# A hybrid decoder layer: normed rows and convolution channels turned from SBUF instead of through DRAM, and one tile's rows loaded into other buffers

## The chip, the core and the metric

The kernel runs on one core of a Trainium2 chip. The metric is the device time of one execution in microseconds (us); the time before is the median of three runs. The profile is one further execution of the same program, taken by the hardware profiler. Engines: PE is the matrix engine (TensorE), PEld its weight load, DVE the vector engine, ACT the scalar engine, POOL GpSimd; SP has no arithmetic here, it issues most of the DMAs. "SPq" and "ACTq" in the rows are DMA issues on the SP and ACT instruction streams. All data are 32-bit floats.

## The reference

One decoder layer on x with 2048 tokens and 1024 channels. What is computed, with the names of the stages that the kernel gives them:

```python
hn = rms_norm(x, mix_pre_g)                     # A
q, k, v, u = split(hn @ w_in)                   # A: 14 column blocks of 128
attn = sliding_window_attention(q, k, v, ...)   # B: window 128, 8 heads, sinks, bias
a, gate = split(u)                              # A
c = depthwise_conv31(a * sigmoid(gate))         # C, "taps": 31 taps, causal
c = silu(layer_norm(c, g, b))                   # C, "tail"
mixed = concat([attn, c @ w_conv_pw]) @ w_out   # W (w_conv_pw @ w_out is folded first, U)
h = x + rms_norm(mixed, mix_post_g)             # W, N
hn = rms_norm(h, ffn_pre_g)                     # N, then turned to channels-first, H
ff = (silu(hn @ w_gate) * (hn @ w_up)) @ w_down # F, then G
out = h + rms_norm(ff, ffn_post_g)              # G
```

layer_norm is over the 512 convolution channels of a token, rms_norm over the 1024 channels of a token.

## The kernel before, in words

**Tiles.** The 2048 tokens are four tiles t = 0 to 3 of 512. A weight or an activation is held as a pair (high part rounded to the fast matmul format, low part the rest), and each product is three matmuls (`three`, line 182; `product`, line 874). The feed-forward part is a seven-product scheme over pairs of tiles, first (0, 1), then (2, 3): names F0, G0, H0 in the code belong to the pair (0, 1), F2, G2, H2 to (2, 3).

**Order of the work.** The program writes its instructions from one main generator at a time (`run`, line 1345); each `yield c` of it lets the side generators in eight "lanes" (`Lane`, line 1267) advance by c times their rate, so that their instructions get their place among the main ones. The lanes that matter here: `lc` the taps T0 to T3 (with a priority that lies 100 places behind), `ld` the tails C0 and C1, `lw` the stages W0, then C2, W2, C3, W3, `lb` the attention B0 to B3, `lh` the turned operands H. The main line is A0, A1, A2, A3, then W1 with the first eight products of F0 inside it (`Q0`, line 1328), then F0, G0, F2, G2. `schedule_with_timeline_sim=True` (line 1493) then fixes the order of each engine's instructions at compile time; on the chip each engine runs its list in that order, and an instruction that waits holds all behind it on its engine. That holds for DMA issues on SP and ACT too.

**Buffers.** `BUFS` (line 53) gives each tag its number of SBUF buffers. Those that the change touches: `fc` 3 (512 values per partition; convolution values), `yt` 1, `chl` 5, `wx` 1, `mb` 2 (one holds the attention bias until B3 ends), `gb` 2, `fa` 4, `at` 2. In PSUM, `ct` is one bank, `tr` three, `mm` four. A new tile waits until the last reader of the buffer's former tile is done, a DMA from it included.

**Convolution.** `stage_taps` (line 554): for each of four channel blocks, 31 DVE instructions on one `fc` tile y, then SP stores y to DRAM (`y_scr`, line 565). `stage_tail` (line 568) loads each block back into an `fc` tile (line 577), turns it on PE to tokens-first in four 128x128 transposes into `ct` (line 549), and ACT copies it into the one `yt` tile (line 550). `conv_tail` (line 583) does the layer norm on `yt` in place (line 597), turns it back per channel block into `ct` (line 601), and makes two `fc` tiles from it: th = tanh (line 603) and v (line 605); DVE joins them (line 606), and SP stores v to `mixT` (line 607).

**Mixing products.** `stage_w(w)` (line 693) loads rows of `mixT` for tile w (`acts`, lines 699 to 711: group 0 is the attention half, the last group the convolution half), splits them into pairs on ACT (line 708) and DVE, and multiplies. For W1 both groups are loaded into `yt`, one 1 MB load each. Its products lie in `mm@W` (W0, W1) or `tr@W` (W2, W3).

**Norm and turn.** `norm_w` (line 747) makes h and the normed rows: xs, four `chl` tiles of 128 tokens x 1024 channels (line 781), which ACT stores to `hn_scr` (line 783). `stage_h_plain` (line 824) later loads a 512-token x 128-channel column block of them (`load_cols`, line 786, pieces of 512 bytes), turns it on PE into `ct` (line 810), scales it on ACT into a `gb` tile u (line 830), stores u to `hT` by a DMA issued on ACT (line 831), and splits u into a pair (lines 833 and 834), the operand `B11` (k = 0 to 3) or `B21` (k = 4 to 7) of the products. It runs for the even tile of each pair, 0 and 2. `stage_h_sums` (line 837) does the other operands: it loads u from `hT`, and the odd tile's blocks from `hn_scr` through `tr` banks.

Of the kernel before, what the change touches and what calls it, by code (L numbers as in the profile page):

```python
# [12 lines left out]
F32 = mybir.dt.float32  # L13
# [4 lines left out]
AF = mybir.ActivationFunctionType  # L18
ALU = mybir.AluOpType
# [6 lines left out]
P = 128  # L26
T = 512
NT = S // T
KC = D // P
# [8 lines left out]
def layer_kernel(ctx, tc, x, xT, cols, rows, sinks, relb, onehot, w_in, w_pw, w_out, w_gate, w_up, w_down, out):  # L38
    nc = tc.nc
# [15 lines left out]
    def t_(tag, shape, dt=F32):  # L55
        return sb.tile(list(shape), dt, tag=tag, name=nm(tag), bufs=BUFS[tag])
# [4 lines left out]
    def f2(tag, shape=(P, T)):  # L61
        return t_(tag, shape)
# [178 lines left out]
    glu_scr = dr.tile([4, P, S], F32, name="glu_scr")  # L241
    hn_scr = dr.tile([S, D], F32, name="hn_scr")
    y_scr = dr.tile([4, P, S], F32, name="y_scr")
    qs = {}
    started = set()

# [298 lines left out]
    def turner(yt, ycs):  # L545
# [5 lines left out]

        return turn

    def stage_taps(t):
        L = f"C{t}"
        for c in range(4):
            while f"g{t}{c}" not in started:
                yield None
            lab[0] = L
            g, y = conv_in(t, c)  # L560
            for j in range(1, TAPS):
                stt(y, g[:, j : j + T], dwh[:, c, j : j + 1], y, ALU.mult, ALU.add)
                yield 0.68
                lab[0] = L
            nc.sync.dma_start(y_scr[c, :, t * T : (t + 1) * T], y)
            yield 0.68

    def stage_tail(t):
        L = f"C{t}"
        lab[0] = L  # L570
        yt = t_("yt", (P, 4, 4 * P))
        ycs = []
        turn = turner(yt, ycs)
        for c in range(4):
            lab[0] = L
            y = f2("fc")
            nc.sync.dma_start(y, y_scr[c, :, t * T : (t + 1) * T])
            ycs.append(y)
            turn(c)
            yield 0.5  # L580
        yield from conv_tail(t, yt)

    def conv_tail(t, yt):
        L = f"C{t}"
        lab[0] = L
        mv = sm(8).rearrange("p (s a) -> p s a", a=2)
        for s in range(4):
            st = sm(6)
            nc.vector.bn_stats(st, yt[:, s])
            nc.vector.bn_aggr(mv[:, s], st)  # L590
        r = rsqrt(mv[:, :, 1], 4, 1.0)
        nmr = sm(4)
        stt(nmr, mv[:, :, 0], -1.0, r, ALU.mult, ALU.mult)
        yield YL if t < 2 else YL2
        lab[0] = L
        for s in range(4):
            act(yt[:, s], yt[:, s], AF.Identity, scale=r[:, s : s + 1], bias=nmr[:, s : s + 1])
        for c in range(4):
            b = ct()
            for s in range(4):  # L600
                nc.tensor.transpose(b[:, s * P : (s + 1) * P], yt[:, s, c * P : (c + 1) * P], ident)
            th = f2("fc")
            act(th, b, AF.Tanh, scale=lnh[:, c : c + 1], bias=lnh[:, 4 + c : 5 + c])
            v = f2("fc")
            act(v, b, AF.Identity, scale=lnh[:, c : c + 1], bias=lnh[:, 4 + c : 5 + c])
            stt(v, th, 1.0, v, ALU.add, ALU.mult)
            nc.sync.dma_start(mixT[4 + c, :, t * T : (t + 1) * T], v)
            yield YZ
            lab[0] = L

# [82 lines left out]
    def stage_w(w, atag, htags, rtags, bank_of, norm=None, ready=None):  # L693
        G = KC // len(htags)
        L = f"W{w}"
        lab[0] = L
        acc = [f4(atag) for _ in range(4)]

        def acts(gi):
            aa = []  # L700
            lab[0] = L
            n = 4 if rtags[gi] == "yt" else 2
            for c in range(G * gi, G * gi + G, n):
                ms = t_(rtags[gi], (P, n, T))
                nc.sync.dma_start(ms, mixT[c : c + n, :, w * T : (w + 1) * T].rearrange("c p t -> p c t"))
                for j in range(n):
                    a = hl(htags[gi])
                    act(a[:, 0], ms[:, j], AF.Copy)
                    vtt(a[:, 1], ms[:, j], a[:, 0].bitcast(F32), ALU.subtract)
                    aa.append([a])  # L710
            return aa

        def weights(gi, n):
            ws = []
            for c in range(G * gi, G * gi + G, 2):
                if c < 4:
                    ws += weight(w_out[c : c + 2, :, n * T : (n + 1) * T].rearrange("c p t -> p c t"), lo_out[n, c : c + 2], w > 0, on_pool=False)
                else:
                    for j in range(2):
                        ws.append(hl("w"))  # L720
                        nc.sync.dma_start(ws[-1].bitcast(F32), fold[n, c - 4 + j])
            return ws

        nxt = acts(0)
        yield W_LEAD
        for gi in range(KC // G):
            aa = nxt
            for n in range(2):
                lab[0] = L
                if n == 1 and gi + 1 < KC // G and not (ready and G * gi + G == 4):  # L730
                    nxt = acts(gi + 1)
                ws = weights(gi, n)
                yield from block_half(acc, list(zip(aa, ws)), n, gi == 0, L, bank_of)
            if ready and G * gi + G == 4:
                for i, c in enumerate(ready()):
                    if i == Q0 // 2:
                        ld.until("C1")
                        lab[0] = L
                        nxt = acts(gi + 1)
                    yield c  # L740
        tail = norm_w(w, acc)
        if norm:
            norm(tail)
        else:
            yield from tail

    def norm_w(w, acc):
        L = f"W{w}"
        lab[0] = L

        def whole(src):
            t = f4("chl")
            nc.sync.dma_start(t, src)
            return t

        gb = whole(rows[0].partition_broadcast(P))
        ssq = sm(4)
        for s in range(4):
            act(junk, acc[s], AF.Square, accum_out=ssq[:, s : s + 1])
            yield 0.75  # L760
            lab[0] = L
        r = rsqrt(ssq, 4, D, w < 3)
        xs = [whole(x[w * T + s * P : w * T + (s + 1) * P]) for s in range(4)]
        ssq2 = sm(4)
        yield 3
        for s in range(4):
            lab[0] = L
            stt(acc[s], acc[s], r[:, s : s + 1], gb, ALU.mult, ALU.mult)
            yield 1.25
            lab[0] = L  # L770
            vtt(acc[s], xs[s], acc[s], ALU.add)
            r0 = w * T + s * P
            nc.sync.dma_start(h_scr[r0 : r0 + P], acc[s])
            act(junk, acc[s], AF.Square, accum_out=ssq2[:, s : s + 1])
            yield 1.25
        lab[0] = L
        r2 = rsqrt(ssq2, 4, D, w < 3)
        yield 3
        for s in range(4):
            lab[0] = L  # L780
            act(xs[s], acc[s], AF.Copy, scale=r2[:, s : s + 1])
            r0 = w * T + s * P
            nc.scalar.dma_start(hn_scr[r0 : r0 + P], xs[s])
            yield 1.25

    def load_cols(w, k, tag):
        t = f2(tag, (P, 4, P))
# [18 lines left out]
    def turned(w, k, bank_of, tag):  # L806
        c = load_cols(w, k, tag)
        b = bank_of()
        for s in range(4):
            nc.tensor.transpose(b[:, s * P : (s + 1) * P], c[:, s], ident)  # L810
        return b
# [12 lines left out]
    def stage_h_plain(ws, ops, n, off):  # L824
        L = f"H{ws[0]}"
        for k in range(4):
            lab[0] = L
            b = turned(ws[0], k + off, ct, COLTAG[ws[0]][k] if ws[0] else "fa")
            u = f2("gb")
            act(u, b, AF.Copy, scale=g_ffn[:, k + off : k + off + 1])  # L830
            nc.scalar.dma_start(hT[ws[0] // 2][k + off], u)
            o = op_tile(ws, ops, n, k, {})
            act(o[:, 0], u, AF.Copy)
            lo(u, o, False)
            yield 2.0
# [509 lines left out]
    def run(gen):  # L1345
        for c in gen:
            clk[0] += c
            for lane in lanes:
                lane.pump(c)
# [52 lines left out]
            hn_a[t + 1] += split_x(t + 1, xa[t + 1][0], xa[t + 1][2], range(4, KC))  # L1402
    lw.until("W0")
    mids = [dr.tile([7, NF // 2, P, T], F32, name=f"mids{i}") for i in range(2)]
    hT = [dr.tile([KC, P, T], F32, name=f"hT{i}") for i in range(2)]
    td = dr.tile([4, NF // 2, P, T], F32, name="td")
    keeps = [dr.tile([PRES[2 * i], P, T], F32, name=f"keeps{i}") for i in range(2)]
    ws, ops = (0, 1), {}
    for n, off in (("B11", 0), ("B21", 4)):
        lh.add(n + ".0", stage_h_plain(ws, ops, n, off))  # L1410
    run(stage_w(1, "mid", ["hl", "chl"], ["yt", "yt"], mm, norm=lambda g: lh.add("N1", g), ready=lambda: stage_pre(ws, ops, mids[0], keeps[0], 0, Q0)))
    lc.hold = lambda: "S0" not in lh.done
    lh.until("B21.0")
    lh.add("S0", stage_h_sums(ws, ops), lambda: f"P0.{PRE_S0}" in started and "B3" in lb.done)
# [83 lines left out]
```

## Time and profile before

| | us |
|---|---|
| median of 3 runs | 1991.65 |
| lowest, highest run | 1988.4, 1992.08 |
| the profiled execution's own time | 1988.67 |
| its span, first to last instruction | 1986.6 |
| PE busy | 1930.2 (97%) |
| DVE busy | 1460.2 (73%) |
| ACT busy | 955.2 (48%) |
| DMA, moved in all | 454.56 MB, mean 229 GB/s |
| mean granted TensorE clock | 0.992 |

How to read it: a matmul of 512 columns is listed with some 390 ns, but successive ones overlap, so the number of matmuls that start in a window says more than their busy time: in an undisturbed 10 us about 46 start. "Idle" of PE is time in which none is in flight. The granted clock in a window is 1.00 when the throttle passes everything. In a row of the time line stand the start, the length, the engine, the line, the operation, out<-in, the count, and in brackets the idle time of the engine just before with what ended it. In a row of waits stand the total, the number and the longest wait. In a row of DMA issues stand the count, the size of one and the median time from issue to landing. A row of windows has the stretch, its length, then for each engine the busy time with the number of instructions, then the granted clock, the DMA engines' busy share and GB/s.

### The profile page before, as it was taken

To read this page: it belongs to the slowest core of one execution; us is meant where nothing else is said; L and a number is where in the kernel's file an instruction comes from. 1 tells how busy PE (TensorE), PEld (TensorE's weight loads), DVE (VectorE), ACT (ScalarE), POOL (GpSimd) and SP (SyncE) were. 2 spreads that over 40 slices of the span, in tenths; PEclk is the share of its full clock that TensorE was granted. 3 is DMA by queue.
4 is the path that set the end of the run, shared out by engine and by line. 5 is a ranking of instruction groups with operands and counts; after the bars stand their busy time and mean duration, and the time that the engine had idled before them with its cause. 6 is when DMAs were issued, how large, how long until landed. Compare 5 with 4: busy or idle time off the path is not lost.

```text
span 1986.6 us, 26669 instructions
## 1 busy us (share of the span) xinstructions
PE 1930.2 (97%) x8730; PEld 1542.3 (78%) x8730; DVE 1460.2 (73%) x2578; ACT 955.2 (48%) x1878; POOL 336.4 (17%) x415
## 2 busy tenths in 40 slices
PE   8999999998999999899999999989999999999997
PEld 6777767776777778778888778768888888888886
DVE  5999969986875898888658975766666665455557
ACT  5455454436737633334355466556634433345443
POOL 4011111003121200000000110144423332311003
PEclk9999999999999999999999999989999999999999
DMA  8797757669659867885477788797844542466664
GB/s 312 253 316 234 228 176 242 213 198 306 203 191 353 290 216 237 285 267 181 154 236 251 266 302 282 270 315 244 289 149 165 170 164 81 143 232 194 210 196 144
DMA packets 229403, 454.56 MB, mean 229 GB/s; under 512 B 22632, under 2 KB 48400, under 8 KB 229264
## 3 DMA queue, kind: packets, MB, share of 16 engines
q1 hardware_dynamic: 211024, 426.64, 64.5%
q10 hardware_dynamic: 18240, 26.22, 3.6%
q8 instruction: 69, 1.13, 0.2%
q14 instruction: 70, 0.57, 0.1%
HBM read 331.65 MB, written 121.12 MB: 228 GB/s over the span
## 4 chain that ended last, share of the span: by engine, by line
PE 43%; DMA 10%; DVE 9%; issue 3%; POOL 2%; ACT 2%; SPq 1%; DVEq 0%; ACTq 0%; POOLq 0%
PE mm@F L85 29%; PE mm@G L85 12%; DVE fc@C L94 2%; PE tr@W L85 2%; DMA gb@F<-keeps 1%; DVE hl@G L94 1%; DMA mids<-fa@F 1%; DMA fa@G<-mids 1%; DMA td<-fc@G 1%; DVE w@F L94 1%; DMA fc@G<-w_down 1%; DMA wx@G<-w_down 1%; DVE fa@F L94 1%; DVE chl@F L94 1%; DMA mixT<-fc@C 1%
## 5 line engine op out<-in xcount | busy, mean ns | idle before, releaser
L94 DVE SCALAR_TENSOR_TENSOR fc@C<-glu@C,colt,fc@C 128x512 f32<-128x512 f32 x480 | 356.5, 760 | 2.9
L85 PE MATMUL mm@F<-hl@H,w@F 128*128 128x512 f32 x1056 | 253.0, 390 | 3.3 <-ACT mm@F L919 2.0
L85 PE MATMUL mm@G<-hl@G,hl@G 128*128 128x512 f32 x924 | 232.6, 397 | 11.2 <-ACT hl@G L792 7.7
L85 PEld LDWEIGHTS mm@F<-hl@H,w@F 128*128 128x128 f32 x1056 | 197.5, 188 | 46.3 <-ACT mm@F L919 3.7
L85 PEld LDWEIGHTS mm@G<-hl@G,hl@G 128*128 128x128 f32 x924 | 173.0, 190 | 51.7 <-ACT hl@G L792 9.0
L85 PE MATMUL mm@A<-hl@A,w@A 128*128 128x512 f32 x840 | 206.5, 395 | 4.2 <-ACT w@A L127 1.9
L792 ACT ACTIVATE w@F<-chl@F 128x512 fp32r<-128x512 f32 x220 | 135.4, 625 | 142.1 <-PE mm@F L85 131.5
L85 PE MATMUL mm@G<-w@G,hl@G 128*128 128x512 f32 x876 | 199.4, 389 | 0.0
L85 PEld LDWEIGHTS mm@G<-w@G,hl@G 128*128 128x128 f32 x876 | 164.4, 188 | 34.1
L85 PEld LDWEIGHTS mm@A<-hl@A,w@A 128*128 128x128 f32 x840 | 155.4, 188 | 42.2 <-ACT w@A L127 2.6
L94 DVE TENSOR_TENSOR w@F<-chl@F,w@F 128x512 fp32r<-128x512 f32 x198 | 144.8, 735 | 35.9 <-ACT w@F L792 35.3
L85 PE MATMUL mm@F<-ql@H,w@F 128*128 128x512 f32 x528 | 128.4, 391 | 9.2 <-ACT mm@F L1026 5.0
L85 PE MATMUL mm@F<-mid@H,w@F 128*128 128x512 f32 x528 | 131.7, 396 | 0.0
L85 PE MATMUL mm@F<-p@H,w@F 128*128 128x512 f32 x528 | 129.4, 390 | 0.0
L85 PE MATMUL mm@F<-x@H,w@F 128*128 128x512 f32 x528 | 125.7, 391 | 0.0
L85 PEld LDWEIGHTS mm@F<-ql@H,w@F 128*128 128x128 f32 x528 | 98.8, 188 | 31.6 <-ACT mm@F L1026 6.4
L494 POOL TENSOR_SCALAR_AFFINE_SELECT p@B<-p@B 128x512 f32<-128x512 f32 x62 | 57.6, 938 | 374.0 <-ACT p@B L492 372.7
L85 PEld LDWEIGHTS mm@F<-mid@H,w@F 128*128 128x128 f32 x528 | 100.0, 190 | 21.9 <-ACT fa@F L1047 0.5
L85 PEld LDWEIGHTS mm@F<-p@H,w@F 128*128 128x128 f32 x528 | 99.5, 188 | 21.0 <-ACT at@F L1040 0.2
L85 PEld LDWEIGHTS mm@F<-x@H,w@F 128*128 128x128 f32 x528 | 98.6, 188 | 21.5 <-issue 0.8
L127 ACT ACTIVATE w@A<-raw@A 128x512 fp32r<-128x512 f32 x110 | 67.4, 625 | 93.5 <-PE mm@A L85 54.8
L94 DVE TENSOR_TENSOR w@G<-raw@G,w@G 128x512 fp32r<-128x512 f32 x73 | 51.5, 705 | 68.1 <-ACT w@G L792 66.8
(302 smaller groups left out, 3300.6 us busy)
## 6 DMA issues: line engine op xcount, KB each, us to landing
mids<-fa@F SPq DMA_DIRECT2D x154, 256.0 KB, 2.8
raw@A<-w_in SPq DMA_DIRECT2D x55, 512.0 KB, 4.7
w@A<-lo_in SPq DMA_DIRECT2D x84, 256.0 KB, 3.6
fc@G<-mids SPq DMA_DIRECT2D x77, 256.0 KB, 3.5
fa@G<-mids SPq DMA_DIRECT2D x75, 256.0 KB, 4.6
gb@F<-keeps SPq DMA_DIRECT2D x72, 256.0 KB, 3.9
w@W<-fold SPq DMA_DIRECT2D x32, 512.0 KB, 5.1
chl@F<-w_gate SPq DMA_DIRECT2D x22, 512.0 KB, 4.1
```

The costliest lines, as they stand in the source:

```text
L85: r = nc.tensor.matmul(*args, **kw)
L94: r = op(*args, **kw)
L127: act(w[:, 0], raw, AF.Copy)
L494: nc.gpsimd.affine_select(out=pg[:, kb].rearrange("p (i q) -> p i q", q=P), in_=pg[:, 1].rearrange("p (i q) -> p i q", q=P), compare_op=AL ...
L792: act(w[:, 0], x, AF.Copy)
```

## The change

Four things are altered.

1. **Convolution channels, tiles 0 and 1.** `stage_taps` no longer stores y to DRAM: as soon as a channel block's taps are done, it turns y into the `yt` tile (taken at the tile's first block, `turns[t]`), in the `lc` lane. `stage_tail(0)` and `(1)` then start with the layer norm. Tiles 2 and 3 still go through `y_scr`.
2. **The tail's values.** In `conv_tail`, for all tiles, v is written into the slice of `yt` that it came from, not into an `fc` tile; the store to `mixT` reads from there, four pieces of 512 bytes per partition.
3. **Normed rows, tiles 0 and 2.** They are no longer stored to `hn_scr` and loaded back in columns. For tile 0 `stage_h_plain` turns them straight from the `chl` tiles, by the new `turn_row`, and `lh.until("B21.0")` in W1 sees to it that this is placed before W1's second group takes `chl` tiles. For tile 2 `norm_w` itself turns all eight blocks and stores them to `hT`, with 2.0 of lane time each, and `stage_h_plain` loads u from `hT`.
4. **Tile 1's rows.** W1's first group goes into a `wx` and an `mb` tile, 512 KB each; the second stays in `yt`.

```diff
--- before.py
+++ after.py
@@ -241,6 +241,7 @@
     glu_scr = dr.tile([4, P, S], F32, name="glu_scr")
     hn_scr = dr.tile([S, D], F32, name="hn_scr")
     y_scr = dr.tile([4, P, S], F32, name="y_scr")
+    hT = [dr.tile([KC, P, T], F32, name=f"hT{i}") for i in range(2)]
     qs = {}
     started = set()
 
@@ -551,6 +552,8 @@
 
         return turn
 
+    turns = {}
+
     def stage_taps(t):
         L = f"C{t}"
         for c in range(4):
@@ -562,12 +565,20 @@
                 stt(y, g[:, j : j + T], dwh[:, c, j : j + 1], y, ALU.mult, ALU.add)
                 yield 0.68
                 lab[0] = L
-            nc.sync.dma_start(y_scr[c, :, t * T : (t + 1) * T], y)
+            if t < 2:
+                if c == 0:
+                    turns[t] = t_("yt", (P, 4, 4 * P))
+                turner(turns[t], {c: y})(c)
+            else:
+                nc.sync.dma_start(y_scr[c, :, t * T : (t + 1) * T], y)
             yield 0.68
 
     def stage_tail(t):
         L = f"C{t}"
         lab[0] = L
+        if t < 2:
+            yield from conv_tail(t, turns[t])
+            return
         yt = t_("yt", (P, 4, 4 * P))
         ycs = []
         turn = turner(yt, ycs)
@@ -601,10 +612,11 @@
                 nc.tensor.transpose(b[:, s * P : (s + 1) * P], yt[:, s, c * P : (c + 1) * P], ident)
             th = f2("fc")
             act(th, b, AF.Tanh, scale=lnh[:, c : c + 1], bias=lnh[:, 4 + c : 5 + c])
-            v = f2("fc")
-            act(v, b, AF.Identity, scale=lnh[:, c : c + 1], bias=lnh[:, 4 + c : 5 + c])
-            stt(v, th, 1.0, v, ALU.add, ALU.mult)
-            nc.sync.dma_start(mixT[4 + c, :, t * T : (t + 1) * T], v)
+            v = yt[:, :, c * P : (c + 1) * P]
+            four = lambda a: a.rearrange("p (s c) -> p s c", c=P)
+            act(v, four(b), AF.Identity, scale=lnh[:, c : c + 1], bias=lnh[:, 4 + c : 5 + c])
+            stt(v, four(th), 1.0, v, ALU.add, ALU.mult)
+            nc.sync.dma_start(four(mixT[4 + c, :, t * T : (t + 1) * T]), v)
             yield YZ
             lab[0] = L
 
@@ -701,7 +713,7 @@
             lab[0] = L
             n = 4 if rtags[gi] == "yt" else 2
             for c in range(G * gi, G * gi + G, n):
-                ms = t_(rtags[gi], (P, n, T))
+                ms = t_(rtags[gi][c // 2 % 2] if isinstance(rtags[gi], tuple) else rtags[gi], (P, n, T))
                 nc.sync.dma_start(ms, mixT[c : c + n, :, w * T : (w + 1) * T].rearrange("c p t -> p c t"))
                 for j in range(n):
                     a = hl(htags[gi])
@@ -735,6 +747,7 @@
                 for i, c in enumerate(ready()):
                     if i == Q0 // 2:
                         ld.until("C1")
+                        lh.until("B21.0")
                         lab[0] = L
                         nxt = acts(gi + 1)
                     yield c
@@ -779,9 +792,28 @@
         for s in range(4):
             lab[0] = L
             act(xs[s], acc[s], AF.Copy, scale=r2[:, s : s + 1])
-            r0 = w * T + s * P
-            nc.scalar.dma_start(hn_scr[r0 : r0 + P], xs[s])
+            if w % 2:
+                r0 = w * T + s * P
+                nc.scalar.dma_start(hn_scr[r0 : r0 + P], xs[s])
             yield 1.25
+        if w == 0:
+            normed.extend(xs)
+        if w == 2:
+            for k in range(KC):
+                turn_row(w, xs, k)
+                yield 2.0
+
+    normed = []
+
+    def turn_row(w, xs, k):
+        lab[0] = f"H{w}"
+        b = ct()
+        for s in range(4):
+            nc.tensor.transpose(b[:, s * P : (s + 1) * P], xs[s][:, k * P : (k + 1) * P], ident)
+        u = f2("gb")
+        act(u, b, AF.Copy, scale=g_ffn[:, k : k + 1])
+        nc.scalar.dma_start(hT[w // 2][k], u)
+        return u
 
     def load_cols(w, k, tag):
         t = f2(tag, (P, 4, P))
@@ -825,10 +857,12 @@
         L = f"H{ws[0]}"
         for k in range(4):
             lab[0] = L
-            b = turned(ws[0], k + off, ct, COLTAG[ws[0]][k] if ws[0] else "fa")
-            u = f2("gb")
-            act(u, b, AF.Copy, scale=g_ffn[:, k + off : k + off + 1])
-            nc.scalar.dma_start(hT[ws[0] // 2][k + off], u)
+            if ws[0]:
+                u = f2(COLTAG[ws[0]][k])
+                nc.sync.dma_start(u, hT[ws[0] // 2][k + off])
+            else:
+                u = turn_row(0, normed, k + off)
+                lab[0] = L
             o = op_tile(ws, ops, n, k, {})
             act(o[:, 0], u, AF.Copy)
             lo(u, o, False)
@@ -1402,13 +1436,12 @@
             hn_a[t + 1] += split_x(t + 1, xa[t + 1][0], xa[t + 1][2], range(4, KC))
     lw.until("W0")
     mids = [dr.tile([7, NF // 2, P, T], F32, name=f"mids{i}") for i in range(2)]
-    hT = [dr.tile([KC, P, T], F32, name=f"hT{i}") for i in range(2)]
     td = dr.tile([4, NF // 2, P, T], F32, name="td")
     keeps = [dr.tile([PRES[2 * i], P, T], F32, name=f"keeps{i}") for i in range(2)]
     ws, ops = (0, 1), {}
     for n, off in (("B11", 0), ("B21", 4)):
         lh.add(n + ".0", stage_h_plain(ws, ops, n, off))
-    run(stage_w(1, "mid", ["hl", "chl"], ["yt", "yt"], mm, norm=lambda g: lh.add("N1", g), ready=lambda: stage_pre(ws, ops, mids[0], keeps[0], 0, Q0)))
+    run(stage_w(1, "mid", ["hl", "chl"], [("wx", "mb"), "yt"], mm, norm=lambda g: lh.add("N1", g), ready=lambda: stage_pre(ws, ops, mids[0], keeps[0], 0, Q0)))
     lc.hold = lambda: "S0" not in lh.done
     lh.until("B21.0")
     lh.add("S0", stage_h_sums(ws, ops), lambda: f"P0.{PRE_S0}" in started and "B3" in lb.done)
```

## The prediction

> **What bounds the kernel now.** I read the page first, for the bound and the chain of work that ended last.
>
> ```profile
> span 1986.6 us, 26669 instructions
> PE 1930.2 (97%) x8730; PEld 1542.3 (78%) x8730; DVE 1460.2 (73%) x2578; ACT 955.2 (48%) x1878; POOL 336.4 (17%) x415
> ...
> PEclk9999999999999999999999999989999999999999
> ...
> PE 43%; DMA 10%; DVE 9%; issue 3%; POOL 2%; ACT 2%; SPq 1%; DVEq 0%; ACTq 0%; POOLq 0%
> ```
>
> The matrix engine is the bound: it sits idle for only 1986.6 - 1930.2 = 56.4 us. The change leaves every matmul and every transpose in place, so it can win only from these 56 us and from stretches in which PE's clock was cut. I therefore looked, by windows of 10 us, for where PE loses.
>
> ```profile
> 480.00:490.00 10.00, 5.87 (x37) 4.62 (x35) 6.27 (x11) 4.53 (x8) 0.00 (x0) 0.90 1.04 398
> 490.00:500.00 10.00, 8.55 (x39) 7.13 (x40) 9.96 (x33) 2.99 (x9) 0.00 (x0) 0.76 0.82 247
> ...
> 810.00:820.00 10.00, 5.97 (x20) 4.46 (x19) 8.14 (x15) 2.67 (x5) 0.00 (x0) 0.83 0.91 328
> 870.00:880.00 10.00, 6.21 (x22) 4.76 (x21) 9.65 (x17) 1.67 (x3) 0.00 (x0) 0.85 0.78 255
> 1310.00:1320.00 10.00, 3.50 (x13) 2.56 (x12) 4.05 (x7) 4.62 (x12) 4.60 (x8) 0.70 1.08 368
> 1320.00:1330.00 10.00, 10.00 (x42) 8.07 (x42) 9.20 (x16) 5.65 (x12) 9.50 (x16) 0.79 0.62 193
> 1350.00:1360.00 10.00, 10.00 (x46) 8.28 (x45) 9.79 (x19) 4.62 (x10) 4.96 (x5) 1.00 0.62 194
> ```
>
> The last row is the undisturbed rate. Two holes lie where the change works: 480 to 500 (A3 gives way to W1) and 1310 to 1330 (tile 2's turned operands). The pair at 810 and 870 lies in F0, which the change doesn't touch. In each of the four the clock falls below 1.00, so a hole costs more than its idle time. The first costs (10 - 5.87) + (10 - 8.55) = 5.6 us idle, and by clock 0.10 x 5.87 + 0.24 x 8.55 = 2.6 us: **8.2 us**. The second costs 6.5 us idle and 0.30 x 3.50 + 0.21 x 10 = 3.2 us: **9.7 us**.
>
> The Trainium skill (TensorE: Matmul & The Clock Gate, the HAM clock gate) says that after an idle window of about 3.4 us the clock halves until about 3.4 us of work have passed; that would be about 1.7 us a hole as an estimate. By it the sum below would gain some 2 us less. The clock rows here give 2.6 and 3.2.
>
> The time line tells what ended the first hole:
>
> ```profile
> 480.55 0.37 SPq L705 DMA_DIRECT2D yt@W<-mixT  x1
> 483.66 0.55 DVE L94 TENSOR_SCALAR fc@C<-glu@C,colt 128x512 f32<-128x512 f32 x1 [7.43 <-DMA mixT<-fc@C]
> 484.78 1.08 PE L85 MATMUL tr@B<-kz,ql@A 64*128 64x256 f32 x13
> 490.69 2.19 ACT L708 ACTIVATE hl@W<-yt@W 128x512 fp32r<-128x512 f32 x4 [4.69 <-DMA yt@W<-mixT]
> 491.45 1.65 PE L85 MATMUL tr@B<-kz,ql@A 64*128 64x256 f32 x12 [5.59 <-DVE sm@B L454]
> 493.03 7.45 PE L85 MATMUL mm@W<-w@W,hl@W 128*128 128x512 f32 x28
> ```
>
> PE ends the projections and a part of B3's scores at 485.86 and then stands before the next scores, which wait for DVE. DVE is late because a tap's first instruction stood 7.43 us before a free `fc` tile: the tail C1 had all three, and one was still being stored to `mixT`. W1 would not have filled the hole either: its rows go into `yt`, which C1 held, so the load was issued at 480.55 and ACT split it at 490.69. Both causes are buffer waits, and DMA is full (1.04).
>
> The second hole:
>
> ```profile
> 1304.05 1.44 SPq L1133 DMA_DIRECT2D mb@G<-w_down  x2
> 1305.54 0.47 SPq L1129 DMA_DIRECT2D fa@G<-mids  x1
> 1306.06 0.45 SPq L1102 DMA_DIRECT2D chl@G<-h_scr  x1
> 1306.99 4.83 PE L85 MATMUL mm@G<-hl@G,hl@G 128*128 128x512 f32 x20
> 1308.79 0.67 ACT L830 ACTIVATE gb@H<-ct@H,colt 128x512 f32<-128x512 f32 x1
> 1315.01 0.33 ACTq L831 DMA_DIRECT2D hT<-gb@H  x1
> 1315.38 0.63 ACT L1094 ACTIVATE junk<-p@G 128x512 bf16<-128x512 f32 x1 [5.92 <-DMA chl@G<-h_scr]
> 1318.33 8.49 PE L85 MATMUL mm@G<-hl@G,hl@G 128*128 128x512 f32 x24 [6.50 <-ACT hl@G L792]
> ```
>
> ACT ends u at 1309.46, then its store to `hT` isn't issued until 1315.01, held by the `chl@G` load of 1306.06. Behind that store in ACT's order stand the splits `hl@G` that PE waits for.
>
> **The change part by part.** The DMAs, from the issues with size and landing time, and the rows for the moved steps:
>
> ```profile
> hn_scr<-chl@W ACTq DMA_DIRECT2D x16, 512.0 KB, 6.7
> y_scr<-fc@C SPq DMA_DIRECT2D x16, 256.0 KB, 3.3
> fc@C<-y_scr SPq DMA_DIRECT2D x16, 256.0 KB, 4.8
> mixT<-fc@C SPq DMA_DIRECT2D x16, 256.0 KB, 5.2
> hT<-gb@H ACTq DMA_DIRECT2D x16, 256.0 KB, 4.4
> fa@H<-hn_scr SPq DMA_DIRECT2D x8, 256.0 KB, 6.0
> ```
> ```profile
> PE ct@C L549 <- DMA fc@C<-y_scr: 1.4, 2, 1.0
> ```
> ```profile
> SPq L565 <- DVE fc@C L94: 25.7, 12, 4.5
> ```
> ```profile
> L491 PE MATMUL tr@B<-ident,p@B 128*128 128x128 f32 x128 | 20.3, 278 | 0.0
> ...
> L810 PE MATMUL ct@H<-ident,fa@H 128*128 128x128 f32 x32 | 5.3, 279 | 0.0
> ```
> ```profile
> 284.06 0.61 DVE L94 TENSOR_SCALAR fc@C<-glu@C,colt 128x512 f32<-128x512 f32 x1 [5.69 <-DMA mixT<-fc@C]
> ```
> ```profile
> L810 PE MATMUL ct@H<-ident,fa@H x32: 270/272/329, 500.7 to 545.3; 128*128 128x128 f32 x32
> L830 ACT ACTIVATE gb@H<-ct@H,colt x16: 668/684/692, 503.4 to 1308.8; 128x512 f32<-128x512 f32 x16
> ```
> ```profile
> L85 PE MATMUL mm@W<-w@W,chl@W x96: 387/389/496, 560.2 to 587.2; 128*128 128x512 f32 x96
> ```
>
> *Traffic.* Gone are 8 stores of 512 KB to `hn_scr`, 16 column loads, 8 stores and 8 loads of `y_scr` at 256 KB; new are 8 loads from `hT`. That is 4 + 4 + 2 + 2 - 2 = 10 MB of 454.56. At the mean of 229 GB/s it is some 45 us of transfer, but PE is the bound, so I count it at nothing by itself; it thins the queues at just the two holes, where DMA reads 1.04 and 1.08. PE's 64 + 64 transposes and ACT's copies stay, only moved.
>
> *W1's rows and the tail's values (first hole).* `wx` is W0's and long done with; `mb`'s second buffer is free too. Their loads need not wait for C1, so I expect them to land well before 485, and W1's products to stand ready when A3 ends. With v in `yt`, C1 needs one `fc` tile per block rather than two, so the tap takes its tile without the 7.43 us, and the scores come in time. ACT's 2.19 us of splits move ahead into a fuller stretch. Bounds: nothing (something else holds W1) and 8.2 us; I take 7.2, leaving 1 us for a late weight: the cover, both causes lifted at once, is good. The same removal lifts 5.69 us of DVE wait at 284; PE wasn't waiting there, so that counts at nothing, but it gives DVE room.
>
> *Tile 2's rows (second hole).* In the stretch 1300 to 1316 no store of u is left on ACT, so the 5.92 us stand goes. Next late are the loads themselves: `fa@G`, issued at 1305.54, with DMA full. If it takes the 9 us that the load of 1306.06 took, PE starts near 1316 and wins 2.4 us; if it lands in time, the whole 9.7 us go. Between these I take 6. In return `norm_w(2)` gets eight blocks at once near 1175: each has an ACT copy of 0.68 and a DMA issue of 0.33, 8 us of ACT, through the single `ct` bank, and the splits `hl@G` stand behind them. Such turns cost PE no idle so far (0.0 over 32). Bounds 0 and 8 x 0.68 = 5.4; I take 1. The lane time of 16 doesn't move C3: by the code's own costs C2, W2 and the turns end at (26 + 45.6 + 24 + 16) / 1.25 = 89, and T3's taps let C3 start at 124 x 0.68 / 0.9 + 10 = 104.
>
> *Tile 0's rows.* The turn needs no DMA, so B11 and B21 (500.7 to 545.3 now) come earlier. The added order holds W1's second group until `chl` is free; it is used only at 560, so 15 us remain even at the old times: nothing.
>
> *Turns inside the taps.* Eight times PE now waits for DVE itself instead of a load. The two old waits, 1.4 us, go. Behind a waiting transpose stand the projections, so a late tap stops PE. What speaks to its price: PE's transposes of what DVE just made in B cost 0.0 idle over 128; SP, placed at the same taps' ends, waited 25.7 / 12 = 2.1 us each. Bounds 0 and 8 x 4.5 = 36 us. I take 3 us, near the B row, which is PE's own. A second wait, for which the stores of C0 are the row:
>
> ```profile
> L607 SPq DMA_DIRECT2D mixT<-fc@C x4: 319/320/384, 268.8 to 292.4; - x4
> ```
>
> T1's first block finds `yt` with C0 until the last of these has landed, 292.4 + 5.2. An ACT copy placed before that stops the weight splits behind it, and by them PE; the order of the lists should put it later, so I count it within the 3.
>
> *Sum:* -7.2 - 6 - 1.4 + 1 + 3 = -10.6 us against the profiled execution's own 1988.67 (span 1986.6 and 2 us around it): 1978. The median of the runs is 3 us above that execution and the runs spread over 3.7; I add 2: **1980 us**.
>
> **The rivals.**
> *The second hole stays.* ACT's stand only moves: DMA at 1.08 keeps the loads late, or the eight stores near 1175 meet the same kind of hold. For it: the transfers of h, `mids` and `w_down` remain. Then 6 us of gain go: 1986.
> *It doesn't do what it says at W1.* The order of the lists is fixed at compile time; if W1's loads stand behind other SP issues, or B3's scores still wait for DVE, the hole keeps its size, and the second too: -1.4 + 4 on 1988.67, with 2 us as above: about 1993. Against it: two causes would have to return.
> *Slower: PE stands before the taps.* One mechanism, at the eight turns of T0 and T1, in A1 to A3, where DVE runs full. At SP's mean of 2.1 us it costs 17, at its longest 36; it decides from (7.2 + 6 + 1.4 - 1) / 8 = 1.7 us a turn. At 3.3 us it is 26: 1988.67 - 13.6 + 26 + 2 = 2003. For it: SP's waits. Against it: SP is mostly idle and waits wherever it stands; PE has a backlog.
>
> **How the numbers follow.** Forecast 0.45, the second hole stays 0.17 (both faster by over 0.2%, about 4 us, which is what a measurement of this kernel can tell from no change), nothing happens at W1 0.13 (same), slower 0.25. So faster 0.62, same 0.13, slower 0.25. The range: both holes gone whole and the turns for nothing give 1988.67 - 17.9 - 1.4 + 2 = 1971, less the runs' spread of 3.7 is 1967; up to 2002, which takes in the middle cases and the lower half of the slow one. The forecast's own range is 1967 to 1985.
>
> **What would show it.** First hole: no PE idle above 2 us and a clock of 1.00 between A3's end and W1; rows of `wx@W` and `mb@W` landing before. No `fc@C` tap waiting for `mixT`. Second: no `hT` store on ACT near 1300, idle under 3 us. Turns: PE's `ct@C` transposes at the taps with less than 1 us of idle each. The forecast is wrong if PE waits for `fc@C` on DVE add up to over 13 us, if a new hole of over 3.8 us opens near 1175, or if F0's holes at 810 and 870 grow by shifted work.

## The result and the profile after

The changed kernel takes 1998.71 us (median of 11 runs, 1994.5 to 2004.8) against 1989.81 us (11 runs, 1986.41 to 1992.08): ratio 1.0051, 95% interval 1.0038 to 1.0063. It is **slower** by about 9 us, little but clear of the noise, where 10 us faster was forecast. The profiled execution took 1997.41 us.

The page of the changed kernel:

```profile
span 1995.4 us, 26645 instructions
...
PE 1933.4 (97%) x8730; PEld 1547.1 (78%) x8730; DVE 1465.0 (73%) x2578; ACT 952.6 (48%) x1878; POOL 327.0 (16%) x415
...
PE   8999999999998999999999999996999999999997
...
PEclk9999999999999999999999999998999999999999
...
DMA packets 224811, 444.06 MB, mean 223 GB/s; under 512 B 22137, under 2 KB 47905, under 8 KB 224673
```

The 10 MB are gone as reckoned, and PE's work is the same 8730 matmuls. But PE's row has a 6 in its 28th slice, where before no slice but the last is under 8. The windows of the changed kernel (stretch, length, busy time of PE, PEld, DVE, ACT and POOL with instructions, clock, DMA share, GB/s):

```profile
480.00:490.00 10.00, 10.00 (x60) 7.51 (x60) 4.19 (x18) 6.93 (x10) 0.00 (x0) 1.00 0.44 131
490.00:500.00 10.00, 10.00 (x54) 7.87 (x53) 9.93 (x26) 8.77 (x27) 0.00 (x0) 1.00 0.57 172
810.00:820.00 10.00, 10.00 (x46) 8.28 (x45) 9.39 (x16) 4.97 (x10) 0.00 (x0) 1.00 0.87 294
870.00:880.00 10.00, 10.00 (x44) 8.17 (x44) 8.99 (x16) 4.91 (x9) 0.00 (x0) 0.96 0.81 262
1310.00:1320.00 10.00, 10.00 (x46) 8.29 (x45) 9.69 (x17) 3.42 (x7) 0.00 (x0) 1.00 0.75 279
1320.00:1330.00 10.00, 10.00 (x46) 8.29 (x45) 8.11 (x14) 9.08 (x21) 5.68 (x5) 1.00 0.98 351
1350.00:1360.00 10.00, 5.60 (x22) 3.97 (x22) 6.42 (x17) 5.20 (x15) 5.32 (x12) 1.00 0.98 351
1360.00:1370.00 10.00, 8.48 (x30) 6.35 (x30) 9.91 (x16) 5.02 (x12) 6.94 (x8) 0.83 0.98 328
1370.00:1380.00 10.00, 5.70 (x22) 4.48 (x23) 5.04 (x17) 2.65 (x5) 0.00 (x0) 0.83 1.01 321
1380.00:1390.00 10.00, 5.26 (x17) 3.58 (x16) 5.83 (x8) 5.03 (x10) 2.24 (x2) 0.81 1.05 357
1390.00:1400.00 10.00, 7.42 (x24) 5.69 (x24) 4.54 (x4) 4.99 (x10) 5.93 (x5) 0.68 0.74 246
1400.00:1410.00 10.00, 6.13 (x28) 4.72 (x27) 7.74 (x9) 6.39 (x12) 4.68 (x3) 0.83 0.61 195
1410.00:1420.00 10.00, 10.00 (x40) 8.09 (x39) 8.07 (x9) 6.34 (x13) 7.74 (x7) 0.83 0.67 216
```

Both holes of the forecast, 480 to 500 and 1310 to 1330, are filled at full clock, and F0's two at 810 and 870 have no idle time either. A new one has opened at F2's start, from 1350 to 1420. A count in these rows takes in every matmul that has a part in the window, so two neighbouring windows share the one at their border. The rate at which matmuls start undisturbed is nearer 44 in 10 us than 46 (146 in 33.25 us in this kernel's time line from 1316.69 on). From 1350 to 1420, as one window, there are 176 matmuls where 7 x 44 = 308 would be; the 132 missing are 132 x 10 / 44 = **30 us**. Of these 21.4 us are idle time (70 less 48.59 busy). The busy time of each row times what its clock lacks to 1.00 adds up to 8.5 us, which is the rest. DMA's share is 0.98 to 1.05 up to 1390.

Why there? N3, the norm of tile 3, ends much later. These are the last stores of h, in the rows of the tile `h_scr` from 1000 to 1450, first of before:

```profile
L773 SPq DMA_DIRECT2D h_scr<-mid@W x8: 319/320/438, 1145.5 to 1284.0; - x8
L1102 SPq DMA_DIRECT2D chl@G<-h_scr x8: 319/326/479, 1277.4 to 1334.4; - x8
```

and then of the changed kernel:

```profile
L786 SPq DMA_DIRECT2D h_scr<-mid@W x8: 319/320/358, 1135.2 to 1322.3; - x8
L1136 SPq DMA_DIRECT2D chl@G<-h_scr x8: 326/571/1350, 1316.6 to 1369.1; - x8
```

The first store is 10 us earlier, the last 38 us later, and with it all that follows: normed rows, column loads, G0's loads of h and its stores to `out`. F2's first products start 26 us earlier, in the rows of the tile `mm@F` from 1290 to 1400, of before:

```profile
L85 PE MATMUL mm@F<-ql@H,w@F x192: 389/389/497, 1343.2 to 1386.6; 128*128 128x512 f32 x192
```

and of the changed kernel:

```profile
L85 PE MATMUL mm@F<-ql@H,w@F x192: 387/389/628, 1316.7 to 1368.4; 128*128 128x512 f32 x192
```

So that traffic, which had lain ahead of F2, falls on its first products. The delay begins at C3's turns, in PE's time line of before:

```profile
1125.38 0.60 PE L549 MATMUL ct@C<-ident,fc@C 128*128 128x128 f32 x4
1134.69 0.60 PE L549 MATMUL ct@C<-ident,fc@C 128*128 128x128 f32 x4
1139.72 0.60 PE L549 MATMUL ct@C<-ident,fc@C 128*128 128x128 f32 x4
...
1187.14 0.63 PE L549 MATMUL ct@C<-ident,fc@C 128*128 128x128 f32 x4 [0.36 <-DMA fc@C<-y_scr]
```

and in that of the changed kernel:

```profile
1158.62 0.27 PE L812 MATMUL ct@H<-ident,chl@W 128*128 128x128 f32 x1
...
1166.84 0.60 PE L812 MATMUL ct@H<-ident,chl@W 128*128 128x128 f32 x4
...
1201.07 0.60 PE L812 MATMUL ct@H<-ident,chl@W 128*128 128x128 f32 x4
...
1206.75 0.60 PE L550 MATMUL ct@C<-ident,fc@C 128*128 128x128 f32 x4
...
1224.76 0.60 PE L550 MATMUL ct@C<-ident,fc@C 128*128 128x128 f32 x4
```

Before, three of C3's four channel blocks were turned by 1140, and only the fourth waited for its taps. Now all four stand behind tile 2's eight turns, `ct@H`, though the second of them was loaded from 1111.7 on and the first before that:

```profile
1080.70 0.46 SPq L588 DMA_DIRECT2D fc@C<-y_scr  x1
1111.72 0.32 SPq L588 DMA_DIRECT2D fc@C<-y_scr  x1
```

Both use the one `ct` bank.

How late traffic stops PE is seen on ACT, in the changed kernel's time line:

```profile
1370.66 0.59 ACT L975 ACTIVATE fa@F<-mm@F 128x512 f32<-128x512 f32 x1
1378.15 0.33 ACTq L976 DMA_DIRECT2D keeps<-fa@F  x1
1378.52 0.60 ACT L953 ACTIVATE mm@F<-gb@F 128x512 f32<-128x512 f32 x1 [7.27 <-DMA raw@F<-w_up]
```

ACT is done with a partial product at 1371.25, but its store isn't issued until 1378.15. The profile puts the end of the wait down to a load of `w_up`, which SP had issued at 1373.20. Behind the store stands the copy that fills the next bank for PE. PE's waits of the changed kernel from 1345 to 1420 (total, number, longest) name that copy first:

```profile
PE mm@F L85 <- ACT mm@F L953: 10.4, 4, 3.5
PE mm@F L85 <- DVE w@F L94: 5.4, 3, 3.1
PE mm@F L85 <- ACT fa@F L975: 4.7, 2, 2.5
```

### The profile page after: what moved, and what is told of

Read it like the earlier page. It is cut to its first block, busy times and chain, and to the rows that moved or that the text cites. A ratio compares the mean times of both kernels' runs of the same rounds, so it can differ in the third digit from the quotient of the medians.

```text
span 1995.4 us, 26645 instructions
## 1 busy us (share of the span) xinstructions
PE 1933.4 (97%) x8730; PEld 1547.1 (78%) x8730; DVE 1465.0 (73%) x2578; ACT 952.6 (48%) x1878; POOL 327.0 (16%) x415
## 5 line engine op out<-in xcount | busy, mean ns | idle before, releaser
L85 PE MATMUL mm@G<-hl@G,hl@G 128*128 128x512 f32 x924 | 227.7, 392 | 2.9 <-DVE hl@G L94 1.8
L85 PE MATMUL mm@F<-mid@H,w@F 128*128 128x512 f32 x528 | 138.8, 411 | 15.6 <-ACT mm@F L953 10.4
L85 PEld LDWEIGHTS mm@F<-mid@H,w@F 128*128 128x128 f32 x528 | 104.6, 199 | 40.6 <-ACT mm@F L953 11.5
L495 POOL TENSOR_SCALAR_AFFINE_SELECT p@B<-p@B 128x512 f32<-128x512 f32 x62 | 52.3, 853 | 363.4 <-ACT p@B L493 362.0
```

The lines of the kernel that those rows point to most:

```text
L85: r = nc.tensor.matmul(*args, **kw)
L495: nc.gpsimd.affine_select(out=pg[:, kb].rearrange("p (i q) -> p i q", q=P), in_=pg[:, 1].rearrange("p (i q) -> p i q", q=P), compare_op=AL ...
```

## The experiments

All are compared with the kernel before on the same chip. Experiments 6 and 8 and the last two of 9 to 12 ran on another chip than the rest; the kernel before has a median of 1987.03 us there and of 1987.6 and 1987.0 in the others, so medians of different experiments are set side by side below. (The result above has 1989.81 for it.) The first theory was **lane time**: the 16 units that tile 2's turns take in lane `lw`, ahead of C3, make C3 late. Its rival was that other parts cost.

**1. Tile 2 back through `hn_scr`**, from the changed kernel:

```diff
-            if w % 2:
+            if w:
                 ...
                 nc.scalar.dma_start(hn_scr[r0 : r0 + P], xs[s])
-        if w == 2:
-            for k in range(KC):
-                turn_row(w, xs, k)
-                yield 2.0
```
(and `stage_h_plain` turns tile 2's column loads as before)

> The changed kernel with tile 2's normed rows put back on their old way: norm_w(2) stores them to hn_scr and stage_h_plain(2) loads them in columns and turns them; no lane time is added. All else of the change stays. Theory (the 16 units of lane time that tile 2's turns take in the lane ahead of C3 make C3, W3 and N3 some 40 us late, and N3's traffic then falls on F2's start): N3's last h_scr store is back at 1275 to 1290 instead of 1322, no hole at 1350 to 1420, tile 2's old hole near 1310 is back; the first hole's gain stays (PE 11 us ahead at 500), so 1976 to 1983 against 1990 of before. Rival (the turns in the taps or the earlier start of F0 and G0 cost what is lost at the end): 1993 to 2001.

Measured: 1973.41 us, ratio 0.9929 (0.9916 to 0.9942). This kernel is called version 1 below. Tile 2's part costs about 25 us, and the rest of the change gains 14, some 3 us more than the theory's range had. N3's last store stands at 1274.2, just ahead of the range, and the hole at F2's start is gone. The old hole near 1310 is back only in part: there are 110 matmuls from 1300 to 1330, where 3 x 44 = 132 would be.

**2. Tile 2's part alone**, on the kernel before (`turn_row` and the loads of `stage_h_plain(2)` as in the changed kernel):

```diff
+            if w != 2:
                 nc.scalar.dma_start(hn_scr[r0 : r0 + P], xs[s])
...
+        if w == 2:
+            for k in range(KC):
+                turn_row(w, xs, k)
+                yield 2.0
```

> The kernel before with nothing but tile 2's part of the change: its normed rows turned in norm_w(2) with 2.0 of lane time each and loaded from hT later. Theory (lane time): tile 2's hole near 1310 goes, worth up to 10 us, but F2's start is starved as in the changed kernel: slower than before, 1995 to 2010. Rival (the first half of the change costs what is lost): faster than before, 1979 to 1985.

Measured: 2009.09 us, 1.0114 (1.0092 to 1.0137); last store at 1335.1. The two runs name the part, but not what in it costs. The next two try the lane time.

**3. No lane time**, in the changed kernel:

```diff
                 turn_row(w, xs, k)
-                yield 2.0
+                yield 0.0
```

> The changed kernel with the eight turns of tile 2 in norm_w(2) taking no lane time (a yield of 0 instead of 2.0 after each): the same instructions, but C3 is no longer held behind 16 units. Theory (lane time): the turns come in one burst, C3's turns and N3 are back near their old times, the hole of 1350 to 1420 goes, and the gain near 1310 stays: 1967 to 1980. Rival (the eight turns themselves, with ct, eight ACT copies and eight DMA issues on ACT, are what delays or what starves F2): 1993 to 2003. A burst that stalls PE near 1160 for up to 8 x 0.7 us would show there as a hole of its own.

**4. Lane time alone**, in the kernel before at the end of norm_w:

```diff
+        if w == 2:
+            for k in range(KC):
+                yield 2.0
```

> The kernel before with nothing but eight yields of 2.0 at the end of norm_w(2): no instruction is added or taken away, only lane time ahead of C3. Theory (lane time): N3's last h_scr store goes from 1284 to about 1315 to 1325, and its traffic runs into F2's start, which comes at about 1343 here (26 us later than in the changed kernel): 1996 to 2010 against 1990. Rival (lane time does nothing by itself): 1988 to 1992.

Measured: without lane time 1995.54 us, 1.0039 (1.0025 to 1.0053); lane time alone 1986.31 us, 0.9996 (0.9984 to 1.0009), not to be told from the kernel before. The `h_scr` row without lane time:

```profile
L786 SPq DMA_DIRECT2D h_scr<-mid@W x8: 319/320/412, 1136.3 to 1329.0; - x8
```

and of lane time alone:

```profile
L773 SPq DMA_DIRECT2D h_scr<-mid@W x8: 319/319/414, 1141.4 to 1281.7; - x8
```

Both are against the theory: N3 is late without lane time, and on time with it. **The lane theory fell.** The compile-time order pulls a ready instruction ahead of others that were named before it; it can't do so where a buffer is handed out in the order of naming. `ct` is one buffer, C3's tiles in it are named after the eight turns, and these wait for norm_w(2)'s rows. That is the second theory, **bank order**; its rivals are the other things that the turns hold: four `chl` tiles, `gb` buffers, eight DMA issues on ACT.

**5. Eight dead turns in `ct`**, added to version 1 at the end of norm_w(2); they hold no `chl` tile after the first, no `gb` buffer, and store nothing:

```diff
+        if w == 2:
+            for k in range(KC):
+                b = ct()
+                for s in range(4):
+                    nc.tensor.transpose(b[:, s * P : (s + 1) * P], xs[s][:, 0:P] if k == 0 else ident, ident)
+                act(junk[:, 0:T], b, AF.Copy)
+                yield 0.0
```

> The version that puts tile 2's rows back through hn_scr (1973.4), with eight turns through ct added at the end of norm_w(2) whose results go nowhere (the first turns a block of the normed rows, the other seven the identity; ACT copies each into junk). No store, no gb buffer and no chl tile is held by them, no lane time. Theory (ct order): C3's first turn goes from about 1115 to 1190 or later, N3's last h_scr store from 1274 to 1300 to 1320, and F2's start is starved: 1983 to 2000. Rival (what delays C3 is the chl tiles, the stores or gb): 1973 to 1978, the eight turns costing only their 8 x 4 transposes at 0.14 us, 4 us at most.

Measured: 1995.87 us, 1.0037 (1.0023 to 1.0052), 22 us above version 1. C3's turns, in PE's time line of this kernel:

```profile
1201.21 0.60 PE L550 MATMUL ct@C<-ident,fc@C 128*128 128x128 f32 x4
...
1218.30 0.60 PE L550 MATMUL ct@C<-ident,fc@C 128*128 128x128 f32 x4
```

The dead turns alone delay C3 as the change does, and cost nearly the whole 25 us; their 32 transposes by themselves would take 4 us at most. With experiment 7, where the same eight turns with their `chl` and `gb` tiles, copies and issues leave C3 on time, bank order is shown.

**6. One dead turn** instead of eight:

```diff
-            for k in range(KC):
+            for k in range(1):
                 b = ct()
```

> The version with tile 2 through hn_scr (1973.4), with one dead turn through ct at the end of norm_w(2) instead of the eight that cost 22 us. Theory (C3's turns queue behind what is named before them in the one bank, and each turn takes about 5.6 us of it): C3's first turn falls to about 1160 to 1168, its last only from 1177 to some 1185, so N3 is less than 10 us later: 1972 to 1979. Rival (the step costs by being there at all, by the wait for norm_w(2)'s rows, not by the number of turns): C3's last turn after 1200 and 1988 to 1996.

Measured: 1984.05 us, 0.9987 (0.9974 to 1.0000). C3's turns stand at 1167.5 to 1184.0, as the theory has it, but N3's last store at 1286.5 is 12 us later than in version 1, where the theory had under 10, and the time lies between the two ranges: one turn costs 10.6. The loss isn't at F2's start but in G0's end (windows of this kernel):

```profile
1310.00:1320.00 10.00, 5.76 (x28) 4.57 (x26) 6.41 (x12) 3.52 (x8) 2.73 (x5) 0.94 1.02 379
1320.00:1330.00 10.00, 3.28 (x8) 2.60 (x9) 7.04 (x11) 3.75 (x7) 1.65 (x9) 0.50 1.07 366
```

**7. The turns through the three `tr` banks**, in the changed kernel:

```diff
-        b = ct()
+        b = tr() if w else ct()
```

> The changed kernel with tile 2's eight turns in norm_w(2) through the three tr banks instead of the single ct bank; all else is as in the changed kernel. Theory (ct order: a bank is taken in the order in which the program names it, C3's turns are named after the eight, the eight wait for norm_w(2)'s rows at 1158, so C3's first turn falls from 1125 to 1207): C3's turns stand at 1115 to 1180 again, N3's last h_scr store at 1275 to 1290, no hole at 1350 to 1420, and tile 2's hole near 1310 stays away: 1964 to 1976. Rival 1 (the eight stores to hT, the gb buffers or the four chl tiles held for the turns delay C3): C3's turns stay near 1207 and the time at 1993 to 2001. Rival 2 (W3's products now queue behind the turns in tr): W3 late instead, 1980 to 1995.

Measured: 1988.21 us, 1.0006 (0.9993 to 1.0019). C3's turns are back at 1116.0 to 1177.7, and the hole at F2's start is gone, as bank order says. The eight turns take 21 us from first to last, where they took 43 in `ct`. But the time is 12 us above the forecast's upper end. Counted from the start of the span, PE is 41 matmuls ahead of before at 1100, 6 at 1300 and 1 behind at 1350; so most of the lead goes before 1300. From 1140 to 1160 there are 63 matmuls (89 in version 1), from 1270 to 1300 114 (127). Then PE loses again in G0's end, though no store of tile 2 is on ACT there (windows of this kernel):

```profile
1320.00:1330.00 10.00, 6.40 (x20) 4.88 (x21) 8.80 (x15) 2.19 (x4) 4.11 (x8) 0.83 0.90 281
1330.00:1340.00 10.00, 6.72 (x30) 5.26 (x29) 2.36 (x4) 1.15 (x2) 0.00 (x0) 0.99 0.61 237
```

ACT's waits of this kernel from 1295 to 1345 say for what:

```profile
ACT hl@G L824 <- DMA mb@G<-w_down: 19.9, 3, 15.5
```

The old second hole is here with its supposed cause taken away. What ends the wait is a load of `w_down`, among N3's and G0's transfers. Rival 2, W3 behind the turns, has its sign too, and the time is in its range: W3's attention products start at 1185.3 and end at 1216.8, where in version 1 they stand from 1136.8 to 1192.6. How much of the loss is W3's was not separated.

**8. G0's finish without its loads of h**, in the changed kernel:

```diff
-            ht = f4("chl" if L == "G0" else "mid")
-            nc.sync.dma_start(ht, h_scr[rows_])
+            if L != "G0":
+                ht = f4("mid")
+                nc.sync.dma_start(ht, h_scr[rows_])
...
-                stt(halves[n], halves[n], r[:, j : j + 1], ht[:, cs], ALU.mult, ALU.add)
+                stt(halves[n], halves[n], r[:, j : j + 1], halves[n] if L == "G0" else ht[:, cs], ALU.mult, ALU.add)
```

> The changed kernel, with G0's finish (tiles 0 and 1) not loading h: it adds the feed-forward rows to themselves, so the output of these tiles lacks h. This takes 8 loads of 512 KB, 4.2 MB, out of 1316 to 1376, and leaves C3, W3 and N3 as late as they are. Theory (F2's start is starved because DMA is full there and ACT's issues to keeps stand behind older transfers): at the 308 GB/s of that stretch 4.2 MB are 13.6 us, so the hole of 1350 to 1420 shrinks by 8 to 18 us: 1980 to 1991 against 1998.7. Rival (the late operands of tiles 2 and 3 themselves hold PE, traffic or not): 1995 to 2001.

The output of tiles 0 and 1 lacks h in this kernel. Measured: 1984.40 us, 0.9983 (0.9970 to 0.9995), 14 us less than the changed kernel, with N3 as late (last store of h 1326.1, F2's first product 1320.5). From 1350 to 1360 this kernel has

```profile
1350.00:1360.00 10.00, 9.00 (x40) 7.14 (x39) 9.76 (x16) 6.96 (x18) 7.92 (x10) 1.00 0.92 290
```

where 22 matmuls had stood. From 1350 to 1420 there are 246, where 176 had been: half of the hole goes with these loads, by 4.2 MB's worth as reckoned. Late operands alone would have kept it whole. But the edit does more than thin the traffic: it also frees the `chl` tiles that these loads took, and the first load of `chl@H` for F2 is issued at 1320.4 instead of 1374.7. The two weren't separated. The other half, 62 matmuls or 14 us, stays, and not all of it lies where DMA is full:

```profile
1360.00:1370.00 10.00, 6.38 (x30) 4.74 (x28) 9.79 (x16) 5.68 (x13) 9.15 (x13) 0.99 0.64 221
```

PE's longest waits from 1345 to 1420 are there for DVE's part of the weight splits, 4.8 us in all. What the second half is owed to stays open.

**9. to 12. The first half of the change.** Parts of the change alone, on the kernel before: part 4,

```diff
-    run(stage_w(1, "mid", ["hl", "chl"], ["yt", "yt"], mm, ...
+    run(stage_w(1, "mid", ["hl", "chl"], [("wx", "mb"), "yt"], mm, ...
```

part 2,

```diff
-            v = f2("fc")
+            v = yt[:, :, c * P : (c + 1) * P]
```

both, and both with part 1 (that is version 1 with tile 0 put back through `hn_scr`):

```diff
+            if t < 2:
+                ...
+                turner(turns[t], {c: y})(c)
```

> The kernel before with part 4 alone: tile 1's first rows loaded into wx and mb. Theory (the first hole has two causes, yt for W1's rows and the fc tile that the taps want, and W1's products fill PE while the scores wait): wx@W and mb@W land before 480, PE's hole at 480 to 500 goes nearly whole: 1978 to 1984. Rival (both causes are needed, PE's order holds the scores ahead of W1): the 5.6 us idle stay, 1986 to 1990.

> The kernel before with part 2 alone: the tail's v in the slice of yt. Theory: the tap's 7.43 us wait for an fc tile goes, but yt is held until v is stored, so W1's rows land as late as before or later, and a hole of 3 to 8 us stays at 480 to 500: 1984 to 1992. Rival (the fc tile is the only cause of the hole): 1978 to 1983.

> The kernel before with parts 2 and 4 alone: tile 1's first rows in wx and mb, and the tail's v in yt. The prediction gave these two 7.2 us. Theory 1: the hole at 480 to 500 goes and stays won, 1979 to 1985. Theory 2 (what is won at 500 is lost in F0's DMA-bound holes from 620 to 900, as with part 4 alone, since nothing of the traffic has gone): 1986 to 1992.

> The version with tile 2 through hn_scr (1973.4), with tile 0's rows put back on the old way too, so parts 1, 2 and 4 alone. The prediction gave part 3's tile 0 nothing. If that holds: 1971 to 1977. Rival (tile 0's 8 MB less of stores and column loads between 500 and 545 are what lets W1 and F0 keep the gain): 1980 to 1990.

| kernel | median, us | ratio (interval) | matmuls ahead of before at 500 us | at 900 us |
|---|---|---|---|---|
| part 4 | 1990.54 | 1.0010 (0.9998 to 1.0022) | 31 | -15 |
| part 2 | 1995.02 | 1.0035 (1.0022 to 1.0048) | -5 | -45 |
| parts 2, 4 | 1982.93 | 0.9979 (0.9967 to 0.9992) | 47 | 18 |
| parts 1, 2, 4 | 1984.72 | 0.9985 (0.9973 to 0.9997) | 49 | 8 |
| version 1: parts 1, 2, 4 and tile 0 | 1973.41 | 0.9929 (0.9916 to 0.9942) | 56 | 42 |

The last columns compare the matmuls of one window from the start of the span to 500 and to 900; 44 are 10 us. Part 4 alone fills the first hole, as its theory said, and then loses all of it: windows of that kernel,

```profile
490.00:500.00 10.00, 10.00 (x55) 7.99 (x53) 9.79 (x25) 4.40 (x8) 0.00 (x0) 1.00 0.97 293
620.00:630.00 10.00, 6.35 (x22) 4.75 (x21) 3.37 (x5) 7.15 (x13) 0.00 (x0) 0.83 1.01 397
790.00:800.00 10.00, 7.61 (x28) 5.88 (x27) 3.63 (x7) 3.16 (x6) 0.00 (x0) 0.86 0.84 274
```

So the time is close to the rival's (half a us above its range), and the reason isn't: PE's order did not hold the scores ahead of W1. Part 2 alone misses both ranges. It leaves the first hole and makes it longer (31 matmuls from 490 to 500, where 39 stood before, and 41 from 500 to 510, where 52 did), and F0 then costs more too. Together they keep 4 us, in the first theory's range, though F0 takes back most of the lead as the second had it; part 1 adds nothing that can be told. Tile 0's straight turn adds 11 us, as its rival said: it has no hole of its own near 500, but without it PE falls behind from 600 to 650. Parts 1, 2 and 4 there:

```profile
600.00:650.00 50.00, 42.15 (x182) 33.40 (x181) 26.34 (x39) 33.05 (x57) 11.00 (x18) 0.93 0.94 321
```

and version 1:

```profile
600.00:650.00 50.00, 44.64 (x208) 35.66 (x207) 31.79 (x48) 36.64 (x65) 14.72 (x20) 1.00 1.01 345
```

That the place is in DMA's fullest stretch is in the rows. The expectation reckoned with 8 MB less for tile 0; it is half of that, 4.2 MB (450.35 to 446.16), the stores and loads from 480 to 515 in the kernel with parts 1, 2 and 4. By what path their absence, or the earlier operands, help at 600 was not tried.

C3 and N3 in one table, from the rows of `ct@C`, `h_scr` and `mm@F`:

| kernel | C3's turns, first and last | last store of h | F2's first product | median, us |
|---|---|---|---|---|
| before | 1125.4, 1187.1 | 1284.0 | 1343.2 | 1989.81 |
| lane time alone | 1121.4, 1183.3 | 1281.7 | 1336.9 | 1986.31 |
| version 1 | 1115.3, 1176.9 | 1274.2 | 1329.4 | 1973.41 |
| turns through `tr` | 1116.0, 1177.7 | 1282.9 | 1343.4 | 1988.21 |
| one dead turn | 1167.5, 1184.0 | 1286.5 | 1339.0 | 1984.05 |
| eight dead turns | 1201.2, 1218.3 | 1318.8 | 1320.6 | 1995.87 |
| changed, no lane time | 1211.2, 1227.6 | 1329.0 | 1320.9 | 1995.54 |
| changed | 1206.8, 1224.8 | 1322.3 | 1316.7 | 1998.71 |
| tile 2's part alone | 1219.6, 1237.6 | 1335.1 | 1329.5 | 2009.09 |

The four kernels of this table with eight turns in `ct`, and only these, store h after 1310 and have the hole at F2's start. **Version 1 beats both kernels**: the one before by 0.7% (0.6 to 0.8), the changed one by 25 us.

## Why the prediction was wrong, step by step

**The step that failed** is tile 2's turns in norm_w(2): "Such turns cost PE no idle so far (0.0 over 32). Bounds 0 and 8 x 0.68 = 5.4; I take 1." It named "the single `ct` bank" and priced only ACT's time in it. It asked what stands behind the turns on ACT, not what is named after them in the same bank: C3. With that the price is 22 us (experiment 5), four times the upper bound. "The lane time of 16 doesn't move C3" was right, as experiment 4 shows, and beside the point.

The Trainium skill (Perfetto Trace Analysis, Matmuls) says that independent groups should rotate through different PSUM banks, so that the copy out of one overlaps the next one's matmuls. The trace agrees: 43 us for the eight turns in one bank, 21 in three. What the single bank holds up behind the turns is the larger price here.

**Second hole, -6:** wrong in its cause. It was laid to the `hT` store held on ACT. In experiment 7 no such store is there, and a hole stays; experiment 5 keeps the store and has none from 1310 to 1330. The rival "the second hole stays" had it right, that the transfers keep the loads late. In the changed kernel the place is filled as N3's traffic comes 38 us later, and there it makes the larger hole.

**First hole, -7.2:** right that it can be filled, and by W1's rows: part 4 alone fills it (31 matmuls or 7 us ahead at 500), the freed `fc` tile alone doesn't, and with both PE is 47 to 56 matmuls (11 to 13 us) ahead. Mis-sized in the end: parts 2 and 4 keep 4 us, since F0 takes back the rest. The prediction reckoned a filled hole as time won at the end; between them lay F0 with limits of its own, as the windows of part 4 alone show (DMA at 1.01 from 620 to 630).

**Tile 0's rows, nothing:** mis-sized. The DMA was counted at nothing since PE is the bound, and the earlier operands too; the step is worth 11 us (1984.72 to 1973.41), by which of the two stays open.

**Turns inside the taps, +3, and the old waits, -1.4:** no effect that can be told (1982.93 and 1984.72, intervals overlapping). In the changed kernel no wait of PE for the taps' `fc@C` on DVE is among its waits, and PE's idle time before all turns of `fc@C` is 0.0, so the slower rival didn't come about. (Of the "64 + 64 transposes" of the prediction 32 of the convolution's move and 64 of the normed rows'; no term rests on it.)

The sum had no term for C3's delay. The change was slower, then, by a mechanism that none of the rivals named. "A new hole of over 3.8 us" was on the list of what would make the forecast wrong, but near 1175; it opened 175 us later.

## What to carry to other kernels

Where a step moves into a buffer or bank of which there is one, list who takes that buffer next in the program's order, when those data would be ready, and who waits for them: a tile that is named earlier and ready later holds back all behind it, whatever the engines are doing. Moving transfers out of a hole in the bound engine can open a larger one where they then fall; follow them there. And a gain is a gain only at the end: count how far the bound engine is ahead after each stage. The changed kernel is 104 matmuls (24 us) ahead of before at 1350 and 38 behind at 1450.

## What the runs showed of the hardware

A DMA issue on ACT stood 6.9 us (1371.25 to 1378.15) with its data ready and, by the profile, was let go as a load that SP had issued at 1373.20 landed; the arithmetic behind it on ACT waited as long. For what it stood, the profile doesn't show. In the hole at F2's start 21.4 us of idle time became 30 us by the granted clock, which lay between 0.68 and 0.83 for 60 us; the clock's part, 8.5 us, is 0.4 us for each us of idle time.
